# Output tiles spread between the quarter products of a two-layer encoder's feed-forward stages, and another way to the weight sums

## The chip, the core and the metric

The kernel runs on one core of a Trainium2 chip. The engines are TensorE (PE, matmuls; PEld its weight loads), VectorE (DVE), ScalarE (ACT), GpSimd (POOL) and SyncE (SP, which only issues transfers). The metric is the device time of one execution in microseconds (us); shorter is better.

## What is computed

Two layers, 512 tokens of width 1024, in fp32. Each layer is a gated feed-forward stage, a mixer of three branches, a cross-attention to 256 memory tokens, and a second feed-forward stage. Cut to the part at hand:

```python
def swiglu(h, w_in, w_out):
    a, b = jnp.split(h @ w_in, 2, axis=-1)
    return (jax.nn.silu(a) * b) @ w_out

for l in range(DEPTH):                                   # DEPTH = 2
    x = x + 0.5 * swiglu(rms_norm(x, ffn1_norm[l]), ffn1_w_in[l], ffn1_w_out[l])
    x = x + merged_branches(rms_norm(x, mix_norm[l])) @ w_mix_out[l]
    x = x + cross_attention(rms_norm(x, xattn_norm[l]), rms_norm(mem, mem_norm[l]), ...)
    x = x + 0.5 * swiglu(rms_norm(x, ffn2_norm[l]), ffn2_w_in[l], ffn2_w_out[l])
return rms_norm(x, final_norm)
```

`w_in` has 2 x 2816 columns. A *unit* is 128 columns of a with the 128 of b that belong to them, so a stage has 22 units; there are four such stages.

## The kernel before

x lies transposed in SBUF, 128 rows of the width by 512 tokens in eight tiles. Every fp32 operand of a matmul is split into a high part (a cast on ACT) and a low part (the rest, a subtraction on DVE), and `mm3` (L422) makes one product from three matmuls: high x high, high x low, low x high. For weights `Stream.split` does this, L400 on ACT and L401 on DVE, three uses ahead of TensorE (`LOOK`), into a ring of four buffers; for activations `split_to` does (L552, L553).

A stage is done in four *blocks* (`FB`): first four plain units, then three blocks of three *pairs* of units. After each block its gated products go through `w_out`: eight *output tiles*, one for each 128 rows of x, each added to x on DVE (L755). `gated` (L599) makes a plain unit's gated product: DVE L602, ACT silu L603, POOL L604, DVE L605, split.

A pair is a two-by-two block product done with seven products in place of eight; each is 4 x 2 weight tiles by 256 tokens, and so 24 matmuls. They are named after their weights: S1, A11, A12, S2, S3, A22, S4. The activations' sums are made once a stage in `combos` and `in_place` (L620, L630, splits L552 and L553). The weights' sums are made by transfers that add to what lies in SBUF, issued by POOL: S1 and S3 when the pair is loaded (L377, L378), S2 when the split of S1 has read the buffer, and S4 when that of S2 has (both L407, in the same buffer). A pair's weights come as two chunks of 1 MB. Pairs take turns between two places: the two `stage` buffers, which also hold the weights of output tiles and of all other products, and two slots of their own (`side`). `room` lets a chunk be loaded when a buffer of its place is free. The pair's results are put together by DVE additions (L663), silu (L667), a DVE product (L674) and a split.

Instructions of one engine run in the order in which a scheduler put them when the kernel was built; it starts from the order of the code and pulls work forward by its own estimates. Side tasks are advanced by `tick`, once for each gated unit, pair and output tile. Transfers of one queue (SP's, POOL's) start in order. `mem_stats` (a side task) computes the memory's norm row in the first stage's last block.

Of the kernel before, what the change touches and what calls it, by code (L numbers as in the profile page):

```python
# [14 lines left out]
P = 128  # L15
# [10 lines left out]
FB = ((4, 0), (0, 3), (0, 3), (0, 3))  # L26
# [45 lines left out]

def plan():

    out = []

    def add(key, parts, make):
        out.append((key, parts, make))

# [12 lines left out]
    def ffn(l, w_in, w_out):  # L92
        j = 0
        for b, (nc, npair) in enumerate(FB):
            j0 = j
            for _ in range(nc):
                first = l == 0 and j == 0 and w_in == "ffn1_w_in"
                add((w_in, l, j), [256, 256, 512, 1024] if first else [1024, 1024], block(w_in, l, 0, KD, (j * P, D_FF + j * P), P))
                j += 1
            for i in range(npair):  # L100
                a, g = (j * P, j * P + P), (D_FF + j * P, D_FF + j * P + P)
                side = (npair - i) % 2
                add((w_in, l, "P", j, side), [2048], blocks(w_in, l, [(0, c) for c in a] + [(4, c) for c in a]))
                add((w_in, l, "Q", j, side), [2048], blocks(w_in, l, [(4, c) for c in g] + [(0, c) for c in g]))
                j += 2
            for m in range(KD):
                add((w_out, l, b, m), [(j - j0) * P], block(w_out, l, j0, j - j0, (m * P,), P))
# [46 lines left out]
    return out  # L154


def pack(w):

    f = {n: np.asarray(a) for n, a in w.items()}
    wts = np.concatenate([np.ascontiguousarray(mk(f)).reshape(-1) for _, _, mk in plan()])  # L160
# [116 lines left out]
def emit(tc, wts, par, rows, ws_t, bd, xt, memt, const, out):  # L277
    nc = tc.nc
    pe, act, dve, pool, sp = nc.tensor, nc.scalar, nc.vector, nc.gpsimd, nc.sync
    chunks = plan()  # L280
# [37 lines left out]
    class Stream:  # L318
# [4 lines left out]

        PAIR = ("S1", "A11", "A12", "S2", "S3", "A22", "S4")

        def __init__(self):
            self.parts = []
            off = 0
            self.off = []
            for i, (key, cols, _) in enumerate(chunks):  # L330
                self.off.append(off)
                off += sum(cols) * P
                if key[2:3] == ("P",):
                    self.parts += [(i, nm, 1024) for nm in self.PAIR]
                elif key[2:3] != ("Q",):
                    c0 = 0
                    for n in cols:
                        self.parts.append((i, c0, n))
                        c0 += n
# [5 lines left out]
            self.slots = None  # L345
# [38 lines left out]
        def source(self, i, nm):  # L384

            p, q = self.loaded[i], self.loaded[i + 1]
            if nm in ("S1", "S2", "S4"):
                return self.xs[self.side(i)].f
# [1161 lines left out]
```

## Time and profile before

| | |
|---|---|
| time, median of 3 runs | 2733.13 us (2726.06 to 2738.3) |
| the profiled execution | 2724.87 us, its span 2723.0 us |
| PE busy | 2609.5 us (96%), 14790 matmuls |
| DVE busy | 1712.8 us (63%) |
| ACT busy | 1306.0 us (48%) |
| POOL busy | 398.5 us (15%) |
| granted TensorE clock, mean | 0.978 of full speed |

The span is the time from the first to the last instruction of the profiled execution. Busy shares are means over the whole span; the stages differ, and the rows below go by stages. In a timeline row the bracket gives the engine's idle time before the instruction and what ended it. PEclk is the clock that was granted to TensorE, 1.00 being the full 2.4 GHz and 0.50 the lower level.

### The profile page before, as it was taken

What the parts mean: (1) busy time and instruction counts of PE and PEld (TensorE: products, weight loads), DVE (VectorE), ACT (ScalarE), POOL (GpSimd) and SP (SyncE); (2) the same over time, 40 slices, a digit from 0 to 9 for tenths busy, and PEclk for the clock granted to TensorE, in tenths of its full rate; (3) what the DMA queues carried; (4) which work ended last, traced back from release to release, by engine and by line L of the source; (5) the groups of instructions that cost most, each with busy time, mean ns of one, the idle gap of its engine ahead of it and who ended that gap; (6) DMA issues with size and microseconds to landing.
All of it is one profiled execution on the core that took longest, in us unless ns stands there. A gap on an engine that the chain in (4) does not pass through costs nothing. (4 is left out here: it accounts for less than half of the span.)

```text
span 2723.0 us, 36733 instructions
## 1 busy us (share of the span) xinstructions
PE 2609.5 (96%) x14790; PEld 2286.3 (84%) x14790; DVE 1712.8 (63%) x2400; ACT 1306.0 (48%) x1829; POOL 398.5 (15%) x366
## 2 busy tenths in 40 slices
PE   8988999999999999899998989999999999999898
PEld 6978988878888889798888889887888888897897
DVE  7646576776656576555675556767675655765555
ACT  5333356876634444332443334579575444433334
POOL 1101134100121021011111101251000300210111
PEclk9989999999999999899999999999999999998999
DMA  5756542222233336566627666322223333376662
GB/s 187 181 153 172 150 149 85 70 78 78 89 105 124 130 106 155 154 163 172 173 74 173 176 151 156 124 86 65 90 78 95 107 125 116 101 182 160 165 150 79
DMA packets 85146, 349.11 MB, mean 128 GB/s; under 512 B 9072, under 2 KB 14832, under 8 KB 66800
## 3 DMA queue, kind: packets, MB, share of 16 engines
q1 hardware_dynamic: 63520, 269.18, 29.1%
q0 software_dynamic: 20736, 75.51, 16.0%
q8 instruction: 115, 1.88, 0.3%
q10 hardware_dynamic: 720, 2.09, 0.2%
q14 instruction: 55, 0.45, 0.1%
HBM read 344.65 MB, written 2.10 MB: 127 GB/s over the span
## 5 line engine op out<-in xcount | busy, mean ns | idle before, releaser
L423 PE MATMUL ps<-slot,whi 128*128 128x256 f32 (+1 forms) x2438 | 829.8, 341 | 80.7 <-ACT slot L552 52.3
L425 PE MATMUL ps<-slot,wlo 128*128 128x256 f32 (+1 forms) x2438 | 825.5, 339 | 6.4 <-DVE wlo L401 6.4
L424 PE MATMUL ps<-slot,whi 128*128 128x256 f32 (+1 forms) x2438 | 827.4, 339 | 1.2 <-DVE slot L553 1.2
L400 ACT CAST whi<-stage 128x1024 fp32r<-128x1024 f32 (+3 forms) x410 | 388.2, 952 | 586.6 <-PE ps L424 381.6
L423 PE MATMUL ps<-xh,whi 128*128 128x512 f32 (+1 forms) x1760 | 597.9, 340 | 5.6 <-DVE slot L1196 3.3
L401 DVE TENSOR_TENSOR wlo<-stage,whi 128x1024 fp32r<-128x1024 f32 (+3 forms) x410 | 466.2, 1139 | 215.3 <-ACT whi L400 213.4
L425 PE MATMUL ps<-xh,wlo 128*128 128x512 f32 (+1 forms) x1760 | 594.5, 338 | 1.1 <-DVE wlo L401 1.1
L424 PE MATMUL ps<-xl,whi 128*128 128x512 f32 (+1 forms) x1760 | 594.8, 338 | 0.3 <-DVE xl L487 0.3
L423 PEld LDWEIGHTS ps<-slot,whi 128*128 128x128 f32 x2438 | 474.4, 195 | 134.4 <-ACT slot L552 57.8
L425 PEld LDWEIGHTS ps<-slot,wlo 128*128 128x128 f32 x2438 | 474.0, 194 | 55.1 <-DVE wlo L401 8.8
L424 PEld LDWEIGHTS ps<-slot,whi 128*128 128x128 f32 x2438 | 474.4, 195 | 52.6 <-DVE slot L553 6.3
L400 ACT CAST whi<-slot 128x1024 fp32r<-128x1024 f32 x204 | 212.0, 1047 | 438.5 <-DMA slot<-in_wts 246.3
L401 DVE TENSOR_TENSOR wlo<-slot,whi 128x1024 fp32r<-128x1024 f32 x204 | 248.6, 1222 | 262.2 <-ACT whi L400 262.0
L423 PEld LDWEIGHTS ps<-xh,whi 128*128 128x128 f32 x1760 | 334.4, 190 | 43.5 <-DVE slot L1196 4.9
L425 PEld LDWEIGHTS ps<-xh,wlo 128*128 128x128 f32 x1760 | 334.4, 190 | 36.8 <-DVE wlo L401 1.7
L424 PEld LDWEIGHTS ps<-xl,whi 128*128 128x128 f32 x1760 | 334.5, 190 | 35.6 <-DVE xl L487 1.6
L552 ACT CAST slot<-slot 128x512 fp32r<-128x512 f32 (+2 forms) x165 | 106.2, 651 | 198.5 <-DVE slot L674 87.9
L755 DVE SCALAR_TENSOR_TENSOR x<-ps,x 128x512 f32<-128x512 f32 x129 | 87.8, 685 | 167.1 <-PE ps L425 166.9
L663 DVE TENSOR_TENSOR slot<-ps,slot 128x512 f32<-128x512 f32 x252 | 168.5, 684 | 24.1 <-PE ps L425 23.2
L407 POOL DMA_DIRECT2D slot<-in_wts x72 | 65.3, 907 | 701.0 <-DVE wlo L401 700.0
L553 DVE TENSOR_TENSOR slot<-slot,slot 128x512 fp32r<-128x512 f32 (+2 forms) x165 | 124.2, 761 | 43.2 <-ACT slot L552 42.2
L553 DVE TENSOR_TENSOR slot<-ps,slot 128x512 fp32r<-128x512 f32 (+1 forms) x144 | 92.6, 654 | 39.3 <-ACT slot L552 38.6
(208 smaller groups left out, 2639.4 us busy)
## 6 DMA issues: line engine op xcount, KB each, us to landing
stage<-in_wts SPq DMA_DIRECT2D x92, 1024.0 KB, 4.8
slot<-in_wts POOLq DMA_DIRECT2D x132, 512.0 KB, 6.2
slot<-in_wts SPq DMA_DIRECT2D x48, 1024.0 KB, 6.2
stage<-in_wts SPq DMA_DIRECT2D x77, 512.0 KB, 3.5
stage<-in_wts SPq DMA_DIRECT2D x96, 384.0 KB, 3.4
slot<-in_wts SPq DMA_DIRECT2D x36, 512.0 KB, 3.6
stage<-in_wts SPq DMA_DIRECT2D x33, 256.0 KB, 2.6
stage<-in_wts POOLq DMA_DIRECT2D x12, 512.0 KB, 8.3
```

Of the source, the lines that this page charges most:

```text
L400: mark["whi"] = act.copy(hi[:, 0:n], t).ins
L401: dve.tensor_tensor(lo[:, 0:n], t, hi[:, 0:n].bitcast(F32), op=ALU.subtract)
L407: pool.dma_start(out=t, in_=self.dram(i, int(c0 == "S2")), accum_op=ALU.add)
L423: pe.matmul(ps, lhsT=ah, rhs=bh, start=start, stop=False)
L424: pe.matmul(ps, lhsT=ah, rhs=bl, start=False, stop=False)
L425: pe.matmul(ps, lhsT=al, rhs=bh, start=False, stop=stop)
L552: act.copy(hi, src)
L553: return dve.tensor_tensor(lo, src, hi.bitcast(F32), op=ALU.subtract).ins
L663: dve.tensor_tensor(r.f, ps, other.f, op=op)
L755: dve.scalar_tensor_tensor(x[:, m, cs], ps, 0.5, x[:, m, cs], op0=ALU.mult, op1=ALU.add)
```

## The change

A stage's order is now a list, `ffn_order`: four plain units, two of their output tiles, then nine pairs in blocks of three, two, two and two. The remaining output tiles of a block stand between the products of the next block's pairs, two to a pair in the first three pairs (after S2 and A22), four to a pair after that (after A11, S2, S3 and A22). The last block's eight tiles stand alone at the end. There are five blocks of output tiles in place of four, 40 additions to x a stage in place of 32, and the same matmuls. The weights of two output tiles come in one chunk.

Pairs no longer use the stage buffers. Three slots hold six buffers of 128x1024: X0 and X1 (in turns by pair), S3, A11, A12 and A22. `fetch` fills one: S1 and S3 by a transfer from SP and one from POOL that adds, the others by one from SP. In X the sum S1 is made into S2 by a DVE addition of A11 after A11's split, and into S4 by one of A12 after S2's. Each buffer is refilled for the next pair as soon as it has been read. A pair moves 3.5 MB in place of 4.5. In-place splits start when the plain units are done, and all side work of `combos` is drained ahead of the first pair.

```diff
-FB = ((4, 0), (0, 3), (0, 3), (0, 3))
+NPLAIN = 4
+PAIR_BLOCKS = (3, 2, 2, 2)
+AHEAD = 2
+PER_PAIR = (2, 2, 2, 4, 4, 4, 4, 4, 4)
+PRODUCTS = ("S1", "A11", "A12", "S2", "S3", "A22", "S4")
+OUT_AT = {2: ("S2", "A22"), 4: ("A11", "S2", "S3", "A22")}
...
+def ffn_order():
+    o = [("unit", j) for j in range(NPLAIN)] + [("block", 0)]
+    ready = [("out", 0, m) for m in range(KD)]
+    o += [ready.pop(0) for _ in range(AHEAD)]
+    i = 0
+    for b, n in enumerate(PAIR_BLOCKS):
+        for _ in range(n):
+            for nm in PRODUCTS:
+                o.append(("product", i, nm))
+                if nm in OUT_AT[PER_PAIR[i]]:
+                    o.append(ready.pop(0))
+            i += 1
+        assert not ready
+        o.append(("block", b + 1))
+        ready = [("out", b + 1, m) for m in range(KD)]
+    return o + ready
...
         def load(self, parts=None, between=None, eng=sp):
...
-            if chunks[i][0][2:3] == ("Q",):
-                s = self.xs[self.side(i)].f
-                eng.dma_start(out=s, in_=self.dram(i, 1))
-                pool.dma_start(out=s, in_=self.dram(i, 0), accum_op=ALU.add)
-                pool.dma_start(out=t[:, 1024:2048], in_=self.dram(i - 1, 0), accum_op=ALU.add)
...
+            while self.n_load < len(chunks) and self.paired(self.n_load):
+                self.n_load += 1
+
+        def open_pairs(self):
+            self.bufs = [get(4) for _ in range(3)]
+            self.buf = dict(zip(("X0", "X1", "S3", "A11", "A12", "A22"),
+                                (r.f[:, h * 1024:h * 1024 + 1024] for r in self.bufs for h in range(2))))
...
+        def fetch(self, nm):
+            n = self.next[nm]
+            self.next[nm] += 1
+            if n == sum(PAIR_BLOCKS):
+                return
...
+            a11, a12, a22, a21 = (src[:, h * 1024:h * 1024 + 1024] for h in range(4))
+            if nm in ("S1", "S3"):
+                t = self.buf[f"X{n % 2}" if nm == "S1" else nm]
+                sp.dma_start(out=t, in_=a21)
+                pool.dma_start(out=t, in_=a22 if nm == "S1" else a11, accum_op=ALU.add)
+            else:
+                sp.dma_start(out=self.buf[nm], in_={"A11": a11, "A12": a12, "A22": a22}[nm])
 
         def split(self):
...
-            elif pair and c0 in ("S1", "S2"):
-                pool.dma_start(out=t, in_=self.dram(i, int(c0 == "S2")), accum_op=ALU.add)
...
+            elif c0 == "A11":
+                dve.tensor_tensor(x0, x0, self.buf["A11"], op=ALU.add)
+                self.fetch("A11")
+                self.fetch("S1")
+            elif c0 == "S2":
+                dve.tensor_tensor(x0, x0, self.buf["A12"], op=ALU.add)
+                self.fetch("A12")
+            elif c0 in ("S3", "A22"):
+                self.fetch(c0)
...
         def combos():
+            ws.open_pairs()
+            ws.fetch("S1")
...
+            total("S3", b12, b22, ALU.subtract)[0].free()
+            while not done:
                 yield
+            in_place("A11", 0, 0)
+            xn[0].free()
+            yield
+            in_place("A12", 1, 0)
+            total("A22", b21, c2, ALU.subtract)[0].free()
+            t2.free()
+            yield
+            in_place("S4", 1, 1)
...
+        def out_tile(b, m):
...
+                for k in range(nj):
+                    c = slice(k * P, (k + 1) * P)
+                    gh, gl, _ = gs[b][k]
+                    mm3(ps, hi[:, c], lo[:, c], gh[:, cs], gl[:, cs], k == 0, k == nj - 1)
+                dve.scalar_tensor_tensor(x[:, m, cs], ps, 0.5, x[:, m, cs], op0=ALU.mult, op1=ALU.add)
...
+        for kind, i, *rest in FFN_ORDER:
...
+            elif kind == "out":
+                out_tile(i, rest[0])
+            else:
+                if rest[0] == PRODUCTS[0]:
+                    if i == 0:
+                        drain()
+                    run = pair()
+                    next(run)
+                run.send(product(i, rest[0]))
```

VectorE's order at the end of the second stage's first block of pairs, before. L663, L674 and L553 finish the last pair, L755 adds output tiles to x, `wlo<-stage` are low parts of output weights:

```order
L663 TENSOR_TENSOR slot_9236<-ps,slot_8237 128x512
L553 TENSOR_TENSOR slot_1767<-slot_8237,slot_1767 128x2x256
L401 TENSOR_TENSOR wlo<-stage,whi 128x768
L674 TENSOR_TENSOR slot_9236<-slot_9236 128x512
L553 TENSOR_TENSOR slot_1767<-slot_9236,slot_1767 128x2x256
L755 SCALAR_TENSOR_TENSOR x<-ps,x 128x512
L401 TENSOR_TENSOR wlo<-stage,whi 128x768
L755 SCALAR_TENSOR_TENSOR x<-ps,x 128x512
L401 TENSOR_TENSOR wlo<-stage,whi 128x768
L755 SCALAR_TENSOR_TENSOR x<-ps,x 128x512
L401 TENSOR_TENSOR wlo<-stage,whi 128x768
L755 SCALAR_TENSOR_TENSOR x<-ps,x 128x512
```

The same place after, in the fourth pair (L754, L778, L603 finish a pair, L728 adds an output tile, L445 splits weights, L456 is one of the new weight sums):

```order
L754 TENSOR_TENSOR slot_8574<-ps,slot_8409 128x512
L445 TENSOR_TENSOR wlo<-slot_8269,whi 128x1024
L778 TENSOR_TENSOR slot_8409<-slot_8409,slot_8574 128x512
L728 SCALAR_TENSOR_TENSOR x<-ps,x 128x512
L445 TENSOR_TENSOR wlo<-stage,whi 128x768
L603 TENSOR_TENSOR slot_9255<-slot_8409,slot_9255 128x2x256
L754 TENSOR_TENSOR slot_8574<-ps,slot_8409 128x512
L445 TENSOR_TENSOR wlo<-slot_8042,whi 128x1024
L778 TENSOR_TENSOR slot_8574<-slot_8574 128x512
L445 TENSOR_TENSOR wlo<-slot_8268,whi 128x1024
L603 TENSOR_TENSOR slot_9255<-slot_8574,slot_9255 128x2x256
L456 TENSOR_TENSOR slot_8268<-slot_8268,slot_8042 128x1024
```

What stood behind the pair, the output tiles and their weights, now stands within the next one, and an addition of 128x1024 has come in.

TensorE's order behind the plain units of the second stage, before, with buffer numbers (`ps_8453`, `ps_8466` and `ps_8510` are the first three output tiles, `slot4_6491` holds the last two units' gated products):

```order
L425 MATMUL ps_8453<-slot4_6491,wlo_8345 128x512
L423 MATMUL ps_8466<-slot4_6491,whi_8386 128x512
L423 MATMUL ps_8453<-slot4_6491,whi_8344 128x512
L424 MATMUL ps_8466<-slot4_6491,whi_8386 128x512
L425 MATMUL ps_8466<-slot4_6491,wlo_8387 128x512
L423 MATMUL ps_8466<-slot4_6491,whi_8386 128x512
L423 MATMUL ps_8510<-slot8_1767,whi_8416 128x512
L424 MATMUL ps_8510<-slot8_1767,whi_8416 128x512
L425 MATMUL ps_8510<-slot8_1767,wlo_8417 128x512
```

After (`ps_8499` and `ps_8522` are the two output tiles ahead of the pairs, `ps_8543` is the first pair's S1, `slot2_7446` holds the last two units' gated products):

```order
L474 MATMUL ps_8522<-slot2_7446,whi_8423 128x512
L475 MATMUL ps_8522<-slot2_7446,wlo_8424 128x512
L473 MATMUL ps_8499<-slot2_7446,whi_8381 128x512
L473 MATMUL ps_8522<-slot2_7446,whi_8423 128x512
L473 MATMUL ps_8543<-slot1_3975,whi_8453 128x256
L474 MATMUL ps_8543<-slot1_3975,whi_8453 128x256
L475 MATMUL ps_8543<-slot1_3975,wlo_8454 128x256
```

Ahead of the low part of the last unit's gated product, which stands in the matmuls of L424, there stood a third output tile, and there now stands part of S1.

## Rows read from the trace of the kernel before

**Rows 1.** Feed-forward stages: length, busy PE, PEld, DVE, ACT, POOL, PEclk, DMA, GB/s.
```profile
7.24:398.63 391.39, 362.06 (x2236) 325.45 (x2237) 251.77 (x323) 163.24 (x215) 53.02 (x53) 0.95 0.61 165
986.44:1367.42 380.98, 356.96 (x2236) 323.50 (x2234) 234.25 (x279) 147.46 (x185) 52.73 (x51) 0.96 0.60 156
1367.42:1744.43 377.01, 357.03 (x2235) 324.09 (x2234) 237.91 (x302) 148.57 (x186) 49.89 (x49) 0.96 0.56 145
2332.16:2705.71 373.55, 353.89 (x2235) 321.45 (x2233) 226.74 (x269) 144.50 (x182) 48.08 (x48) 0.97 0.54 138
```

**Rows 2.** The same view: one pair, eight output tiles, and one low-clock stretch.
```profile
1053.39:1073.54 20.15, 20.15 (x169) 20.15 (x168) 11.45 (x13) 7.95 (x9) 4.31 (x5) 1.00 0.88 222
...
1711.76:1744.43 32.67, 32.67 (x146) 27.04 (x145) 28.00 (x52) 19.66 (x28) 9.18 (x7) 1.00 0.49 161
...
1339.95:1343.35 3.40, 3.40 (x10) 2.62 (x9) 2.90 (x5) 2.90 (x4) 0.66 (x1) 0.50 0.29 88
```

**Rows 3.** Waits of PE over the span: in total, times, longest.
```profile
PE ps L423 <- ACT slot L552: 52.3, 13, 7.8
PE ps L423 <- ACT whi L400: 28.6, 9, 6.3
```

**Rows 4.** Timeline of ACT and PE at one block end (start, length).
```profile
1105.95 1.04 ACT L400 CAST whi<-slot 128x1024 fp32r<-128x1024 f32 x1 [8.42 <-DMA slot<-in_wts]
...
1107.05 0.58 PE L423 MATMUL ps<-slot,whi 128*128 128x256 f32 x1 [4.55 <-ACT whi L400]
...
1127.29 0.83 ACT L400 CAST whi<-stage 128x768 fp32r<-128x768 f32 x1 [9.67 <-DMA stage<-in_wts]
...
1133.90 0.80 PE L423 MATMUL ps<-slot,whi 128*128 128x512 f32 x1 [7.30 <-ACT slot L552]
```

**Rows 5.** DMA issues of the page: KB each, median us to landing.
```profile
slot<-in_wts POOLq DMA_DIRECT2D x132, 512.0 KB, 6.2
```

**Rows 6.** Groups of instructions by line and shape: busy us, mean ns of one.
```profile
L401 DVE TENSOR_TENSOR wlo<-slot,whi 128x1024 fp32r<-128x1024 f32 x204 | 248.6, 1222 | 262.2 <-ACT whi L400 262.0
...
L663 DVE TENSOR_TENSOR slot<-ps,slot 128x512 f32<-128x512 f32 x252 | 168.5, 684 | 24.1 <-PE ps L425 23.2
...
L755 DVE SCALAR_TENSOR_TENSOR x<-ps,x 128x512 f32<-128x512 f32 x127 | 86.9, 689 | 165.7 <-PE ps L425 165.5
...
L553 DVE TENSOR_TENSOR slot<-slot,slot 128x1024 fp32r<-128x1024 f32 x20 | 26.0, 1301 | 3.3 <-ACT slot L552 3.3
```

**Rows 7.** Timeline of PE, VectorE and ACT around the first output tiles, second stage.
```profile
1030.49 0.39 PE L423 MATMUL ps<-slot,whi 128*128 128x512 f32 x1
...
1031.16 0.69 DVE L401 TENSOR_TENSOR wlo<-stage,whi 128x512 fp32r<-128x512 f32 x1 [0.46 <-ACT whi L400]
...
1033.80 0.62 ACT L552 CAST slot<-slot 128x512 fp32r<-128x512 f32 x1 [0.25 <-DVE slot L605]
...
1035.95 0.69 DVE L553 TENSOR_TENSOR slot<-slot,slot 128x512 fp32r<-128x512 f32 x1
...
1036.69 0.50 PE L424 MATMUL ps<-slot,whi 128*128 128x512 f32 x1 [0.34 <-DVE slot L553]
```

**Rows 8.** Timeline of PE and ACT at the third stage's last block.
```profile
1711.76 0.40 PE L423 MATMUL ps<-slot,whi 128*128 128x512 f32 x1
...
1715.57 0.62 ACT L552 CAST slot<-slot 128x512 fp32r<-128x512 f32 x1 [1.10 <-DVE slot L674]
```

**Rows 9.** Timeline of PE, first stage: first output tile, and the memory row.
```profile
56.00 0.39 PE L423 MATMUL ps<-slot,whi 128*128 128x512 f32 x1
...
384.06 0.48 PE L461 MATMUL ps<-slot,ones_r 128*128 128x256 f32 x1 [2.38 <-ACT slot L552]
```

**Rows 10.** Timeline of POOL and VectorE in the first stage's last block.
```profile
393.13 1.52 POOL L496 TENSOR_TENSOR nacc<-nacc,slot 128x512 f32<-128x512 f32 x1 [2.48 <-ACT slot L495]
...
393.42 1.78 DVE L487 SCALAR_TENSOR_TENSOR xl<-x,par,xh 128x512 fp32r<-128x512 f32 x1
...
396.86 0.74 DVE L487 SCALAR_TENSOR_TENSOR xl<-x,par,xh 128x512 fp32r<-128x512 f32 x1
```

More of the change, by code (lines that the diff above doesn't have):

```diff
@@ L1 @@
+from bisect import bisect_left as bisect
 import numpy as np
@@ L70, with add @@
 BRANCH_ORDER = branch_order()
+def ffn_order():
[14 more added lines that the diff above has]
+    return o + ready
+FFN_ORDER = ffn_order()
+BLOCK_AT = [0, NPLAIN]
+for _n in PAIR_BLOCKS:
+    BLOCK_AT.append(BLOCK_AT[-1] + 2 * _n)
 def plan():
-    out = []
-    def add(key, parts, make):
+    out, order = [], []
+    def add(key, parts, make, now=True):
+        i = len(out)
         out.append((key, parts, make))
+        uses = [(i, sum(parts[:k]), n) for k, n in enumerate(parts)]
+        if now:
+            order.extend(uses)
+        return i, uses
     def block(name, l, k0, nk, cols, n):
@@ L607, in gated @@
             t.free()
[L608 removed]
+            gs[-1].append((g.r[:, 0:512], g.r[:, 512:1024], g))
         xn = []
@@ new lines, in combos @@
+            xn[1].free()
+        def out_tile(b, m):
+            nj = BLOCK_AT[b + 1] - BLOCK_AT[b]
+            last = b == len(PAIR_BLOCKS)
+            hi, lo = ws.take((w_out, l, b, m // 2))
+            tail = last and m == KD - 1 and isinstance(nxt, FinalNorm)
+            for h in range(2 if tail else 1):
+                cs = slice(h * 256, h * 256 + 256) if tail else slice(0, 512)
+                ps = bank()[:, 0:cs.stop - cs.start]
+                for k in range(nj):
[3 more added lines that the diff above has]
+                dve.scalar_tensor_tensor(x[:, m, cs], ps, 0.5, x[:, m, cs], op0=ALU.mult, op1=ALU.add)
+                if tail:
+                    nxt.half(h)
+            if last and not tail:
+                nxt.tile(m)
+            if m == KD - 1:
+                for _, _, g in gs[b]:
+                    if g is not None:
+                        g.free()
+            tick(2 if last and norm is first else 1)
@@ new lines, in product, with add @@
+        def product(i, nm):
+            ps = bank()
+            hi, lo = ws.take((w_in, l, "pair", i), nm)
+            mh, ml, _ = mv[nm]
+            for e in range(2):
+                for k in range(4):
+                    c = slice(e * 512 + k * P, e * 512 + (k + 1) * P)
+                    mm3(ps[:, e * 256:(e + 1) * 256], hi[:, c], lo[:, c], mh[k], ml[k],
+                        e == 0 and k == 0, e == 1 and k == 3)
+            return ps
+        def add(ps, other, op=ALU.add):
+            r = get(1)
+            dve.tensor_tensor(r.f, ps, other.f, op=op)
+            return r
@@ L670, in pair, with silu @@
+        def silu(r):
+            mark["silu"] = act.activation(r.f, r.f, AF.Silu).ins
+            return r
+        def pair():
+            p5 = yield
+            q1 = get(1)
+            act.copy(q1.f, (yield))
+            a0 = silu(add((yield), q1))
+            u2 = add((yield), q1, ALU.subtract)
+            w = add(p5, u2, ALU.subtract)
+            q1.free()
+            p7 = yield
+            u3 = add(p7, u2)
+            b1 = add(p7, w, ALU.subtract)
+            u2.free()
             g = getr(4)
```

246 lines of the change are left out of this document (86 added, 160 removed).

## The prediction

> **What bounds the kernel now.** The first view read is that of busy times by stretch, one stretch for each of the four feed-forward stages, in the kernel's order of time [rows 1]. In all four TensorE (PE) is the busiest engine, 362.1 of 391.4 us in the first, and VectorE (DVE) comes second with 251.8. But each has two kinds of loss. PE sits idle for 29.3, 24.0, 20.0 and 19.7 us, 93.0 together, and PEclk, the granted clock, is 0.95 to 0.97, so a part of each stage runs at the lower of the clock's two levels (1.2 of 2.4 GHz).
>
> What such a stage costs without loss follows from two undisturbed stretches [rows 2]: a pair of units takes 20.15 us for 7 x 24 = 168 matmuls of 256 columns, 0.120 us each, and a block of eight output tiles 32.67 us for 144 of 512 columns, 0.227 us each. By the code a stage has 9 x 168 = 1512 of the first kind and 192 + 528 = 720 of the second (four plain units, and output tiles over 22 units in whatever blocks). That is 181.3 + 163.4 = 344.7 us. The four stages last 391.39 + 380.98 + 377.01 + 373.55 = 1522.9; without loss they would last 1378.8. So 144 us are lost, 93 to idle time, 51 to the lower clock. The last row of the group is one stretch at 0.50: 3.40 us, so 1.7 us of work lost. All that the change can win lies in these 144 us: it has the same matmuls.
>
> Then PE's waits [rows 3]: 52.3 us for ACT's split of a gated product (L552), in 13 waits, 28.6 us for ACT's split of weights (L400). One block end shows both [rows 4]. ACT idles 8.42 us for a transfer into a pair buffer (the accumulating one at L407, which can be issued only when the split of the earlier sum has read the buffer), and PE stands 4.55 us behind it. Then ACT idles 9.67 us for the block's output weights, which wait for one of the two stage buffers that the pairs use as well. The last product's additions and splits are queued behind that split on ACT and VectorE, and PE stands 7.30 us.
>
> **The change part by part.** *Weight sums.* S2 and S4 become VectorE additions in SBUF, so the 72 transfers of L407 go, and with them the first kind of stall, the 28.6 us of [rows 3] (9 waits, the longest 6.3). S1 and S3 stay transfers, but S1 has two buffers and is fetched a pair ahead, S3 is fetched when its buffer has been split, a whole pair before its use. An accumulating transfer lands 6.2 us after issue at the median [rows 5]; with the plain one ahead of it about twice that, 12.4. A pair with two output tiles takes 20.15 + 24 x 0.227 = 25.6 us, so I price these waits at nothing. If the cover went, PE would wait as in [rows 4] once a pair (second rival). SP's fetches wait for VectorE's addition or split; behind them in SP's queue stand the output weights, needed by ACT's split three uses later, some 8 us; what SP waits for stands earlier in VectorE's list than the work on those weights, so it does not stand long. POOL's queue holds in this stretch only the remaining transfers.
>
> *VectorE pays for it.* The nearest row for an addition of 128x1024 with two SBUF inputs is the split at 1.30 us [rows 6]. Per pair VectorE then does 7 splits at 1.22 (8.6), 2 additions (2.6), 7 additions from PSUM at 0.684 (4.8), 2 products and 2 splits of 128x512 like the one at 0.69 [rows 7] (2.8), and for two output tiles of four units 2 x (0.69 + 0.69) = 2.8 (such a split and the addition to x): 21.6 of PE's 25.6 us. Three splits are in hand ahead of PE, so I cost this at nothing in the steady pairs. Eight more output additions a stage (40, not 32) are 5.5 us of VectorE, inside the same cover.
>
> *Block ends.* Blocks 0 to 3 now have the next block's products between their output tiles. The last product's chain (4.43 us to its high part, [rows 8]) has the next pair's S1 and A11 before it, 2 x 2.88 us. Output weights have the stage buffers to themselves. These stalls go. What is late next:
>
> First, block 0. Before, the first tiles wait for unit 3's gated product: from the block's start at 1030.49 its high part is there at 3.93 us, its low part at 6.15 us, and PE stood 0.34 us for it [rows 7]. After, ACT splits 1024 columns of pair weights ahead of the silu in place of 512, 1.04 us in place of 0.62 [rows 4, 7], 0.42 later: 4.4 and 6.6. PE has two tiles with 9 matmuls each ahead (4.1 us), then two high products and ten of S1 (0.45 + 1.2), so it idles 0.3 + 0.5 us. Behind that VectorE has three sums and their splits, 3 x (1.22 + 1.30) = 7.6 us by the same rows, before the pair is in step: counting its list up, the low weights of S2 come some 1 us late. I take 2 us a stage; bounds 0 and 4.2 (the low part at 6.6 with one tile's 2.4 us ahead of it).
>
> Second, the last block, which has no pair behind it. There the high part came at those 4.43 us; PE now has 12 to 17 matmuls ahead of it, 2.7 to 3.9 us, in place of 24. I take 1 us a stage, bounds 0 and 1.7. Some of these eight places will also drop the clock; I take half of them, 4 x 1.7 = 7 us in all, bounds 0 and 14.
>
> Third, things that stay: the first stage's start, 48.8 us to 56.00 where 192 x 0.227 = 43.6 would do (5.2 us lost), and the memory statistics' row in its last block, 2.4 us idle [rows 9] and 1.7 for the clock. The last block shrinks from 32.7 to 21.8 us while the layer's small work after it (the recurrence's constants, the next norm) does not: I add 2 us for each first feed-forward stage, bounds 0 and 5.
>
> **The sum.** Left over: 5.2 + 4.1 + 4 x 2 + 4 x 1 + 7 + 4 = 32 us of the 144. The span falls by 112, from 2723.0 to 2611; with the 1.9 us around it (the profiled execution took 2724.9) 2613. That execution was 8.3 us below the median of the runs, so the median should be 2613 + 8 = 2621.
>
> **A rule that speaks against it.** In the first stage's last block a split on VectorE with two SBUF inputs took 1.78 us beside an addition of 1.52 us on POOL, and 0.74 us with POOL at rest [rows 10]. The Trainium skill, in "SBUF — State Buffer", section "Who interferes with whom", says that a VectorE instruction with two SBUF inputs and a GpSimd instruction that reads SBUF exclude one another; the trace agrees. In the new last block a tile lasts 12 x 0.227 = 2.72 us and holds 0.69 + 0.74 of such VectorE work and 1.52 of POOL's, 2.95 together; if they exclude one another, 32 tiles are 0.23 us late each, 7 us. If they do not, nothing is lost. This is a part of the first rival.
>
> **The rivals.** *VectorE becomes the bound.* From unit 3's end to the end of pair 2 PE has 3 x 25.6 + 5.4 = 82 us of work. VectorE has 3 x 21.6 + 7.6 + 4.5 (three operations at 0.69 of unit 3, two in-place splits at 1.22) + 2.8 = 79.7. Against it: 79.7 is still less, and on average it is at 84%. For it: its list is in order and waits for ACT and PE now and then. If it runs 5% over in each stage, 4 x 4 us, and the last block by POOL's 7, and the clock drops twice more a stage (4 x 2 x 1.7 = 14), that is 37 us more: median 2658. Chance 0.22.
>
> *The wait for transfers moves into every pair* (slower). Four buffers, S3, A11, A12 and A22, are single now, where each pair of a block had its own set before; a refill starts only after VectorE has read the buffer and then queues in SP. If one refill a pair comes late by a stall like those of [rows 4], 4.55 us and 1.7 for the clock, 36 pairs lose 225 us in place of 144: median 2733 + 81 = 2814. It decides from some 4 us a pair, that is when a refill needs over 25 us, against 12.4 in the trace, and the bytes per pair fall from 4.5 to 3.5 MB. Chance 0.03.
>
> *Only the transfer stalls go.* If the block ends merely move (the out tiles of a block stand among products which themselves wait in order), the 52.3 us of [rows 3] stay, with a drop of clock for each of 13 waits, 22 us: median 2621 + 74 - 19 (what the sum already has for such places) = 2676. Against it: the products between need nothing of the last pair. Chance 0.06.
>
> **How the numbers follow.** The forecast has 0.69. Faster by over 0.5% (14 us, about what a measurement tells from no change) holds in it and in the first and third rival: 0.97, of which I take 0.02 off for what I have not seen. The low end is the sum with the fixed 5.2 + 4.1 = 9.3 us alone: 2621 - 23 = 2598, less a little. The upper bounds of the four estimated terms (8.8 + 2.8 + 7 + 6 = 25 more) give 2646, the first rival 2658: the high end is 2662.
>
> **What would show it.** In the profile after: PE idle in each stage under 12 us, PEclk 0.98 or more, no wait of ACT for a pair transfer above 2 us; PE's waits for L552's split few, at block 0 and the last block alone; VectorE at about 84% in the first three pairs. PE waiting for VectorE's low weights all through pairs 0 to 2 would speak for the first rival, ACT waiting for transfers in each pair for the second. The forecast is wrong if the four stages together stay above 1450 us.

## The result and the profile after

The changed kernel takes 2608.6 us (median of four runs, 2607.4 to 2610.5) against 2729.6 us for the kernel before (2724.0 to 2738.3). The ratio is 0.9555, 95% interval [0.9526, 0.9583]: 121 us or 4.4% faster. The forecast was 2621 us, in a range from a little under 2598 to 2662. The profiled execution has a span of 2606.5 us.

The stretches of busy time are the rows that answer to [rows 1], one for each feed-forward stage (columns as there):

```profile
7.14:369.86 362.72, 353.56 (x2236) 320.20 (x2237) 273.41 (x340) 165.85 (x221) 35.93 (x34) 0.99 0.51 150
957.84:1305.39 347.55, 346.56 (x2235) 316.63 (x2234) 259.35 (x310) 149.65 (x191) 34.93 (x31) 1.00 0.51 141
1305.39:1654.20 348.81, 346.70 (x2236) 316.66 (x2234) 262.89 (x322) 150.44 (x192) 33.75 (x30) 1.00 0.47 131
2242.64:2589.05 346.41, 345.43 (x2235) 315.78 (x2233) 252.36 (x303) 147.51 (x190) 31.46 (x28) 1.00 0.44 122
```

PE idles 9.2, 1.0, 2.1 and 1.0 us (length less busy time), in place of 93.0 together, and PEclk, the granted clock, is 0.99 to 1.00. The four stages last 1405.5 us in place of 1522.9, 26.7 more than the 1378.8 without loss. VectorE (DVE) does 9 to 11% more in each, and it costs nothing that these rows show.

PE's waits are those of [rows 3] (in total, times, longest). L602 is the split of gated products that was L552, L444 the split of weights that was L400:

```profile
PE ps L473 <- ACT slot L602: 6.9, 6, 2.5
PE ps L511 <- ACT slot L602: 5.6, 2, 3.6
PE ps L473 <- ACT xh L536: 3.3, 2, 1.9
PE ps L473 <- DVE slot L1256: 3.3, 2, 1.6
```

The 52.3 us for the gated split are 6.9, with 0.9 more for its low part on VectorE, and no wait for the split of weights is left. The L511 waits are the memory statistics' row (3.6) and the final norm.

The page's DMA issues (KB each, median us to landing) show what went: the 72 accumulating transfers of L407 are no longer among POOL's, and the pairs' weights come in 180 plain transfers of 512 KB. The 72 that are left are the second halves of S1 and S3.

```profile
slot<-in_wts SPq DMA_DIRECT2D x180, 512.0 KB, 4.2
...
slot<-in_wts POOLq DMA_DIRECT2D x72, 512.0 KB, 6.1
```

### The profile page after: what moved, and what is told of

Same layout as the page of the kernel before. It is cut to its first block, busy times and chain, and to the rows that moved or that the text cites. A ratio compares the mean times of both kernels' runs of the same rounds, so it can differ in the third digit from the quotient of the medians.

```text
span 2606.5 us, 36643 instructions
## 1 busy us (share of the span) xinstructions
PE 2571.5 (99%) x14784; PEld 2260.2 (87%) x14784; DVE 1826.2 (70%) x2536; ACT 1321.3 (51%) x1861; POOL 337.2 (13%) x294
## 4 chain that ended last, share of the span: by engine, by line
PE 90%; ACT 5%; DVE 3%; DMA 1%; POOL 1%; issue 1%; DVEq 0%; ACTq 0%; SPq 0%; POOLq 0%
PE ps L474 29%; PE ps L473 29%; PE ps L475 29%; PE ps L1132 1%; PE ps L1120 1%; PE ps L1103 1%; ACT whi L444 1%; DVE wlo L445 1%; DVE slot L603 0%; DMA x<-in_xt 0%; DVE xl L537 0%; POOL slot L654 0%; ACT L909 0%; ACT L919 0%; PE ps L1433 0%
## 5 line engine op out<-in xcount | busy, mean ns | idle before, releaser
L473 PE MATMUL ps<-slot,whi 128*128 128x256 f32 (+1 forms) x2436 | 812.9, 335 | 6.9 <-ACT slot L602 6.9
L474 PE MATMUL ps<-slot,whi 128*128 128x256 f32 (+1 forms) x2436 | 814.3, 334 | 0.9 <-DVE slot L603 0.9
L475 PE MATMUL ps<-slot,wlo 128*128 128x256 f32 (+1 forms) x2436 | 810.9, 334 | 0.0
L444 ACT CAST whi<-stage 128x1024 fp32r<-128x1024 f32 (+3 forms) x394 | 346.4, 881 | 509.5 <-PE ps L474 412.9
L445 DVE TENSOR_TENSOR wlo<-stage,whi 128x1024 fp32r<-128x1024 f32 (+3 forms) x394 | 415.5, 1056 | 148.0 <-ACT whi L444 145.3
L473 PEld LDWEIGHTS ps<-slot,whi 128*128 128x128 f32 x2436 | 463.1, 190 | 54.0 <-ACT slot L602 10.0
L474 PEld LDWEIGHTS ps<-slot,whi 128*128 128x128 f32 x2436 | 463.7, 190 | 46.0 <-DVE slot L603 2.4
L475 PEld LDWEIGHTS ps<-slot,wlo 128*128 128x128 f32 x2436 | 463.1, 190 | 46.2
L444 ACT CAST whi<-slot 128x1024 fp32r<-128x1024 f32 x252 | 265.3, 1053 | 433.4 <-PE ps L474 318.5
L445 DVE TENSOR_TENSOR wlo<-slot,whi 128x1024 fp32r<-128x1024 f32 x252 | 307.8, 1222 | 66.0 <-ACT whi L444 66.0
L754 DVE TENSOR_TENSOR slot<-ps,slot 128x512 f32<-128x512 f32 x252 | 170.6, 689 | 140.9 <-PE ps L475 139.7
L428 POOL DMA_DIRECT2D slot<-in_wts x72 | 62.9, 874 | 1204.3 <-DMA slot<-in_wts 1053.3
L602 ACT CAST slot<-slot 128x512 fp32r<-128x512 f32 (+2 forms) x165 | 106.0, 649 | 147.3 <-POOL slot L1290 44.6
L728 DVE SCALAR_TENSOR_TENSOR x<-ps,x 128x512 f32<-128x512 f32 (+1 forms) x161 | 110.5, 686 | 88.7 <-PE ps L475 88.6
L603 DVE TENSOR_TENSOR slot<-slot,slot 128x512 fp32r<-128x512 f32 (+2 forms) x165 | 123.0, 754 | 51.7 <-ACT slot L602 51.7
L603 DVE TENSOR_TENSOR slot<-ps,slot 128x512 fp32r<-128x512 f32 (+1 forms) x144 | 92.8, 655 | 38.7 <-ACT slot L602 38.1
```

The source lines that it names most:

```text
L428: pool.dma_start(out=t, in_=a22 if nm == "S1" else a11, accum_op=ALU.add)
L444: mark["whi"] = act.copy(hi[:, 0:n], t).ins
L445: dve.tensor_tensor(lo[:, 0:n], t, hi[:, 0:n].bitcast(F32), op=ALU.subtract)
L473: pe.matmul(ps, lhsT=ah, rhs=bh, start=start, stop=False)
L474: pe.matmul(ps, lhsT=ah, rhs=bl, start=False, stop=False)
L475: pe.matmul(ps, lhsT=al, rhs=bh, start=False, stop=stop)
```

## The experiments

The change has three parts: S2 and S4 summed by VectorE, own buffers for the pairs' weights, and the spread order. What goes with the buffers was not taken apart from them: earlier fetches, output weights two tiles to a chunk, chunks loaded as far ahead as there is room, later in-place splits, side work drained ahead of the first pair. "Own buffers" stands for all of these below. They were undone one at a time and two at a time. "Grouped" is the order of before, three blocks of three pairs, each followed by its eight output tiles.

**The order alone undone** (`grouped`).

```
-PAIR_BLOCKS = (3, 2, 2, 2)
+PAIR_BLOCKS = (3, 3, 3)
...
+    for b, n in enumerate(PAIR_BLOCKS):
+        for _ in range(n):
+            o += [("product", i, nm) for nm in PRODUCTS]
+            i += 1
+        o.append(("block", b + 1))
+        o += [("out", b + 1, m) for m in range(KD)]
```

> The kernel after, with the order of before: three blocks of three pairs, each followed by its eight output tiles (the first two begun on the earlier units), block 0's eight tiles ahead of the first pair. Buffers and weight sums stay those of after. Theory A (own buffers for the pair weights are what ends the block-end waits, since the last product's additions and splits no longer queue behind a split that waits for output weights): the waits for the gated product's split stay away from the ends of blocks 1 and 2, about 2610 to 2630 us, ratio 0.955 to 0.963. Theory B (spreading the tiles is what ends them): 52 us of such waits and 22 us of lower clock come back, about 2676 us, ratio 0.98.

2598.3 us (2598.0 to 2601.0), ratio 0.9522 [0.9508, 0.9537]. Theory B falls: without the spread no block end came back, and the kernel is faster than theory A had it. It is 10 us faster than the changed one. The two were timed apart and the intervals of their ratios overlap a little; kernels of either order that were timed side by side follow below. PE's waits in this trace:

```profile
PE ps L506 <- ACT slot L597: 4.3, 2, 2.9
...
PE ps L468 <- ACT slot L597: 1.3, 4, 0.7
```

L597 is the gated split: 1.3 us where before had 52.3 in the same order of products and tiles.

**The VectorE sums alone undone** (`transfer_sums`).

```
+            elif c0 == "S1":
+                pool.dma_start(out=x0, in_=self.quarter(i, 0), accum_op=ALU.add)
...
-                dve.tensor_tensor(x0, x0, self.buf["A12"], op=ALU.add)
+                pool.dma_start(out=x0, in_=self.quarter(i, 1), accum_op=ALU.add)
```

> The kernel after, with S2 and S4 made by accumulating transfers again, issued when S1 and S2 have been split (72 transfers of 512 KB back, 72 additions of VectorE gone). Order and buffers stay those of after. If the transfers are hidden behind the four splits between (some 11 us for 6.2 us of transfer), the time stays: 2600 to 2615 us, ratio 0.953 to 0.958, and VectorE is 10 points less busy in the first three pairs. If these transfers were a cause of their own, ACT waits for them as before: 28.6 us of PE's waits and half as much for the clock, about 2650 us, ratio 0.971.

2660.1 us, ratio 0.9741 [0.9726, 0.9756]: the transfers are not hidden, and cost a little more than the second case had. The timeline of VectorE, POOL, ACT and PE shows one such place in the second stage (start, length, engine and line, in brackets the idle time before and what ended it):

```profile
1067.88 1.22 DVE L449 TENSOR_TENSOR wlo<-slot,whi 128x1024 fp32r<-128x1024 f32 x1
...
1074.16 0.86 POOL L428 DMA_DIRECT2D slot<-in_wts  x1 [8.64 <-DMA slot<-in_wts]
1074.76 1.15 POOL L456 DMA_DIRECT2D slot<-in_wts  x1
...
1085.83 1.04 ACT L448 CAST whi<-slot 128x1024 fp32r<-128x1024 f32 x1 [12.67 <-DMA slot<-in_wts]
...
1086.93 0.58 PE L479 MATMUL ps<-slot,whi 128*128 128x256 f32 x1 [3.16 <-ACT whi L448]
```

The first row is the low split of S1, done at 1069.1. From then on the sum for S2 (L456) could have been issued. It was issued at 1074.76, because POOL's queue stood 8.64 us at an accumulating fetch (L428) that waits for its plain half. Two accumulating transfers then ran at once. ACT could go on only at 1085.83, 16.7 us after the split, and PE stood 3.16 us behind it.

**Order and sums undone, own buffers kept** (`grouped_transfer_sums`: both edits).

> Both undone at once: the order of before and S2 and S4 by accumulating transfers; only the own buffers for pair weights and the earlier fetches stay of the change. Theory A (own buffers are enough): 2610 to 2640 us, ratio 0.956 to 0.967. Theory B (the spread order removes the block ends, the VectorE sums the transfers' waits): near before, 2690 to 2730 us, ratio 0.985 to 1.0.

2763.4 us, ratio 1.0129 [1.0107, 1.0151]: slower than before, outside both cases. PE's waits:

```profile
PE ps L474 <- ACT whi L443: 85.3, 20, 7.6
PE ps L476 <- DVE wlo L444: 11.2, 21, 0.8
PE ps L474 <- ACT slot L603: 7.0, 9, 2.4
```

They are waits for the split of pair weights, in the middle of blocks, and only 7.0 us are for gated products. The row of events of `transfer_sums` stands here too (POOL):

```profile
1081.11 0.87 POOL L423 DMA_DIRECT2D slot<-in_wts  x1 [6.69 <-DMA slot<-in_wts]
1081.71 1.15 POOL L451 DMA_DIRECT2D slot<-in_wts  x1
```

The split of S1 was done at 1077.6. The transfer for S2 (L451) was issued 4.2 us later, behind a fetch (L423) that had waited for its plain half.

**The VectorE sums alone done** (`before_vector_sums`, on the kernel before).

```
             elif pair and c0 in ("S1", "S2"):
-                pool.dma_start(out=t, in_=self.dram(i, int(c0 == "S2")), accum_op=ALU.add)
+                h = int(c0 == "S2")
+                dve.tensor_tensor(t, t, self.loaded[i][:, h * 1024:(h + 1) * 1024], op=ALU.add)
```

> The kernel before with one edit: S2 and S4 are made by a VectorE addition of A11 and A12, where before accumulating transfers made them. Order and shared buffers of before stay. With it the runs so far form a square: shared or own buffers, transfers or VectorE. If the accumulating transfers behind the splits of S1 and S2 were the whole cause: 2600 to 2620 us, as the grouped order with own buffers (2598), ratio 0.953 to 0.96. If own buffers are needed as well (pairs and output weights still share the stage buffers, ACT waits 124 us for them in before): 2640 to 2690 us, ratio 0.967 to 0.985.

2628.9 us, ratio 0.9654 [0.9627, 0.968], between the two cases. Two lines bring 99 of the change's 119 to 121 us. PE's and ACT's waits, two views:

```profile
PE ps L424 <- ACT slot L553: 18.5, 10, 3.0
```

```profile
ACT whi L400 <- DMA stage<-in_wts: 70.1, 28, 5.1
```

ACT's waits for transfers in the kernel before were these:

```profile
ACT whi L400 <- DMA slot<-in_wts: 246.3, 52, 10.1
ACT whi L400 <- DMA stage<-in_wts: 124.1, 34, 9.7
```

The 246.3 us for pair buffers are gone. The waits for the stage buffers fell too, though the buffers are shared as before. What is left of the block ends is of this kind (ACT and PE, second stage):

```profile
1094.89 0.83 ACT L400 CAST whi<-stage 128x768 fp32r<-128x768 f32 x1 [4.64 <-DMA stage<-in_wts]
...
1098.03 0.50 PE L424 MATMUL ps<-slot,whi 128*128 128x512 f32 x1 [2.70 <-ACT slot L553]
```

It is the second stall of [rows 4] (9.67 and 7.30 us there): the output weights wait for a stage buffer, and PE for the gated split behind them. With own buffers, and what goes with them, it is gone: in `grouped` PE's waits for the gated split are 1.3 us. Together (ratio to before):

| | S2, S4 by transfers | by VectorE |
|---|---|---|
| shared buffers, grouped | 2729 us, 1 (before) | 2628.9, 0.9654 |
| own buffers, grouped | 2763.4, 1.0129 | 2598.3, 0.9522 |
| own buffers, spread | 2660.1, 0.9741 | 2608.6, 0.9555 (after) |

The spread order is worth 103 us where the transfers remain. There PE's waits for the split of weights fall from 85.3 to 12.5 us, while those for gated products rise from 7.0 to 20.2. That the output tiles between a pair's products give the transfers more time fits this, but no run shows it by itself. With VectorE's sums the spread order brings nothing.

**The transfers' wait made on purpose** (`single_x`).

```
-                self.fetch("A11")
-                self.fetch("S1")
+                self.fetch("A11")
...
+            elif c0 == "S4":
+                self.fetch("S1")
```

> The kernel after with one buffer for the sums S1, S2 and S4 in place of two: the next pair's S1 is fetched only when S4 has been split. This makes the wait of the prediction's second rival on purpose: plain and accumulating transfer, some 12 us, against about 8 us of PE's work between the split of S4 and the use of S1. If the price stands as that rival had it, 4 to 5 us and 1.7 us for the clock in each of 36 pairs: 2780 to 2850 us, ratio 1.02 to 1.045. If it is hidden: 2605 to 2620 us, ratio 0.955 to 0.96.

2807.9 us, ratio 1.0291 [1.0274, 1.0309], as the first case had it. It is 199 us over the changed kernel, 5.5 in each of 36 pairs.

```profile
PE ps L474 <- ACT whi L444: 119.9, 39, 9.3
```

**VectorE made dearer** (`vector_plus`; `vector_plus_half` has it for the second sum alone).

```
                 dve.tensor_tensor(x0, x0, self.buf["A11"], op=ALU.add)
+                dve.tensor_tensor(x0, x0, self.buf["A11"], op=ALU.subtract)
+                dve.tensor_tensor(x0, x0, self.buf["A11"], op=ALU.add)
```

> The kernel after with VectorE's weight sums made dearer: each is followed by a subtraction and an addition of the same quarter (2 x 1.22 us more per sum, 4.9 us per pair), the values stay. From the first pair to the end of the third VectorE is busy 72 of 83 us in the second stage of after; 14.7 us more make 86.7. If only the excess over PE's time counts: 3.7 us a stage, 15 in all, 2610 to 2635 us, ratio 0.956 to 0.965. If VectorE's own waits in its ordered list can't be used up, all of it shows: 4 x 14.7 = 59 us, about 2668 us, ratio 0.977. If it has room to spare: 2605 to 2612 us.

> Half the dose: only the second sum of a pair is followed by a subtraction and an addition (2.4 us more per pair). VectorE then has 72 + 7.3 = 79.3 of 83 us in the first three pairs. If only the excess over PE's time counts: no change, 2605 to 2615 us, ratio 0.955 to 0.958. If all of it shows: 4 x 7.3 = 29 us, about 2638 us, ratio 0.966.

2615.0 us, ratio 0.9582 [0.9564, 0.96], and 2610.6 us, ratio 0.9562 [0.9541, 0.9582]: most of the added work is hidden. Both times lie in the ranges of the case in which only the excess over PE's time counts. First the three pairs of the second stage in the changed kernel:

```profile
1011.50:1037.00 25.50, 25.50 (x193) 24.51 (x192) 25.50 (x30) 13.65 (x17) 1.76 (x2) 1.00 0.52 144
1037.00:1063.00 26.00, 26.00 (x197) 25.02 (x196) 20.93 (x26) 11.20 (x14) 1.73 (x2) 1.00 0.74 189
1063.00:1089.00 26.00, 26.00 (x197) 25.02 (x196) 20.06 (x25) 11.19 (x15) 1.73 (x2) 1.00 0.65 176
```

then with the full dose:

```profile
1018.00:1044.00 26.00, 25.39 (x191) 24.18 (x190) 26.00 (x30) 11.83 (x14) 0.88 (x1) 1.00 0.42 122
1044.00:1070.00 26.00, 26.00 (x198) 25.02 (x197) 26.00 (x32) 11.07 (x14) 2.61 (x3) 1.00 0.68 178
1070.00:1096.00 26.00, 26.00 (x198) 25.02 (x197) 25.05 (x31) 12.12 (x16) 1.73 (x2) 1.00 0.70 186
```

VectorE is busy for all of the first pair in the changed kernel, and has room in the two after it (80 and 77%). With the dose it is full for two pairs and 96% busy in the third, and PE loses 0.61 us. So the 59 us that VectorE's list gained in the first three pairs of the four stages (4 x 14.7) moved the time by 6. Of these, 3.9 lie ahead of the pairs: at the first stage's block 0 PE waits 6.48 us for the gated split, where it waited 2.54 in the changed kernel. Two of the added operations (L453, L454) stand in VectorE's list between the steps of the last unit (VectorE and PE, full dose):

```profile
61.86 1.22 DVE L453 TENSOR_TENSOR slot<-slot,slot 128x1024 f32<-128x1024 f32 x1
...
63.60 1.22 DVE L454 TENSOR_TENSOR slot<-slot,slot 128x1024 f32<-128x1024 f32 x1
...
68.33 1.22 PE L477 MATMUL ps<-slot,whi 128*128 128x512 f32 x2 [6.48 <-ACT slot L606]
```

In the steady pairs VectorE sets no end, at block 0 it does.

**Where the spread order loses.** Five kernels looked for the 10 us between the two orders. `spread_from_block1` writes block 0's tiles ahead of the first pair (`OUT_AT` has an empty entry for 0 besides):

```
-AHEAD = 2
-PER_PAIR = (2, 2, 2, 4, 4, 4, 4, 4, 4)
+AHEAD = KD
+PER_PAIR = (0, 0, 0, 4, 4, 4, 4, 4, 4)
```

> The kernel after with all eight output tiles of block 0 ahead of the first pair; later blocks stay spread. Theory C (the 10 us that the spread order costs against the grouped one lie in the two places where it leaves PE too little work: the first tiles of block 0 and the last block): half of it goes, mostly the first stage's 2.54 us gap and 1.7 us of clock and 0.5 to 1 us in each other stage, 2601 to 2605 us, ratio 0.953 to 0.9545. Rival (the spread costs everywhere, by VectorE or transfers beside the tiles): 2606 to 2610 us.

2605.2 us, ratio 0.956 [0.9539, 0.9582]: the two cases meet there, so it decides nothing. Block 0's waits in stages two to four fell from 0.98 to 0.53 us, in the first stage the wait grew to 3.24.

`spread_mended` has two edits more:

```
-OUT_AT = {... 4: ("A11", "S2", "S3", "A22")}
+OUT_AT = {... 4: ("A11", "S2", "A22", "S4")}
...
         split_to(o.r[:, 0:MEM], o.r[:, MEM:2 * MEM], a)
+        yield
+        yield
         row_scale(mem_row, [o.r[:, 0:MEM], o.r[:, MEM:2 * MEM]])
```

> The same, and the last of four tiles of a block behind product S4 rather than A22, so that the last block's first tile has a tile of the block before between it and the last product's additions, and two more steps of the output tiles between the split of the memory statistics and PE's matmul on it (3.55 us of PE's wait in after). Theory C: the waits at the last blocks (1.22 and 1.14 us) and the 3.55 us with 1.7 us of clock go as well, 2593 to 2599 us, ratio 0.950 to 0.9525. Rival (they move to the next place in order): 2600 to 2606 us.

2604.6 us (2602.6 to 2605.6), ratio 0.9554 [0.9533, 0.9576]. The last blocks' waits are gone from the trace, but the memory row kept 3.06 and 1.05 us, and theory C's time was not reached. The same two steps on the grouped order (`grouped_late_row`):

> The kernel with the grouped order, own buffers and VectorE sums (2598.3 us), and the same two steps between the split of the memory statistics and the matmul on it, 2.87 and 0.95 us of PE's waits there. If these waits and the lower clock behind them cost what they show: 2592 to 2595 us, ratio 0.949 to 0.951. If the wait moves on to the row's next use: 2597 to 2599 us.

2597.2 us (2593.9 to 2600.5), ratio 0.953 [0.951, 0.955]: not to be told from `grouped`. The row's waits fell from 2.87 and 0.94 to 1.41 and 1.14 us. It ran beside `spread_mended`, and no run of the one reaches the other: the grouped order is the faster by about 7 us.

Last, the begun tiles. In before the first two output tiles of a block start on its earlier units, and `grouped` had kept that. `grouped_whole_tiles` takes it away:

```
-            if m == 0:
-                for e in range(2):
-                    begun[e] = (bank(), ws.take((w_out, l, b, 0)))
-                    partial(*begun[e], b, whole, range(nj - 2))
...
+            w = ws.take((w_out, l, b, m // 2))
```

> The grouped kernel (2598 us) without the one thing that it shares with before beyond its order: the first two output tiles of a block are no longer begun on the block's earlier units ahead of the last product's results; every tile is written whole. Theory D (a begun tile and a spread tile are two covers for the same 4.4 us between the last product and the high part of its gated units, so that spreading had nothing left to cover): waits at all twelve block ends, some 1 to 1.7 us each and part of them with a drop of clock, 2612 to 2630 us, ratio 0.957 to 0.9635. Rival (the order between matmuls of ready tiles takes care of it anyway): 2597 to 2603 us, ratio 0.951 to 0.954.

2598.6 us (2594.2 to 2599.1), ratio 0.9529 [0.9514, 0.9543]. Theory D falls for the twelve blocks of pairs: no wait of 0.4 us or more stands at their ends. At the first stage's block 0 it holds: `grouped` has 0.73 us there, and without the begun tiles it is this, with a lower clock behind:

```profile
62.21 0.80 PE L468 MATMUL ps<-slot,whi 128*128 128x512 f32 x1 [3.29 <-ACT slot L597]
```

```profile
62.20:65.60 3.40, 3.39 (x8) 2.71 (x9) 3.37 (x4) 0.00 (x0) 0.00 (x0) 0.50 0.03 11
```

The time doesn't show it, and the trace says why: the memory row's waits of 2.87 and 0.94 us are missing in it, so that one loss is made up by another gain. `spread_begun` gives begun tiles to block 0 of the mended spread kernel:

> The mended spread kernel (2604.6 us), with the two begun tiles of before at block 0 alone. If the first stage's block 0 (3.33 us of wait, 1.7 us of clock) is what still parts it from the grouped order: 2596 to 2600 us, ratio 0.950 to 0.9525. If the begun tiles change nothing there: 2603 to 2606 us.

2604.0 us (2599.8 to 2606.7), ratio 0.9547 [0.9531, 0.9563]: they change nothing, and block 0's wait in the first stage stays at 3.35 us. The profiles of these two differ by 9.2 us at the same point behind the first stage (PE's wait for L1258, or L1272, the same instruction), and by under 2 after it. The stretch from 340 to 370 us, which holds the first stage's last block, has most of it; first `grouped_whole_tiles`, then `spread_begun`:

```profile
340.00:370.00 30.00, 30.00 (x135) 24.86 (x134) 27.13 (x45) 17.93 (x28) 13.72 (x12) 1.00 0.35 120
```

```profile
340.00:370.00 30.00, 25.36 (x100) 20.06 (x100) 27.68 (x48) 20.70 (x36) 15.15 (x15) 0.89 0.47 163
```

```profile
362.95 0.58 PE L511 MATMUL ps<-slot,ones_r 128*128 128x256 f32 x1 [3.76 <-ACT slot L602]
364.41 0.58 PE L511 MATMUL ps<-slot,ones_r 128*128 128x256 f32 x1 [0.88 <-DVE slot L603]
```

The memory statistics' matmul has 4.6 us of waits here and a lower clock behind them (a clock of 0.89 over 30 us is 3.3 us of work), 8 us together; in the other it waits for nothing. This is no mark of the order: in `grouped` the same row has 2.87 and 0.94 us with a clock of 0.50 behind, more than the 3.55 us and one drop of the changed kernel.

What parts the changed kernel from `grouped` lies in every stage. From its first output tile to its last, each stage is longer by 4.2, 1.2, 2.4 and 1.3 us (first stage, `grouped`, then the changed kernel):

```profile
56.40:365.90 309.50, 304.61 (x2042) 282.09 (x2041) 237.85 (x291) 137.54 (x175) 29.02 (x29) 0.99 0.52 142
```

```profile
55.93:369.63 313.70, 306.31 (x2042) 282.69 (x2041) 234.92 (x290) 137.84 (x181) 28.03 (x28) 0.99 0.49 137
```

The places where PE idles more are block 0 (2.54 us and a drop of the clock in the first stage, against 0.73) and the last blocks (1.22 and 1.14 us, against less than 0.4). In `spread_mended` the last blocks' waits are gone. Its span is still 7.4 us longer than that of `grouped`, and 5.0 of these have gathered by PE's first wait behind the first stage (for L1256 at 525.13 us, and for the same instruction at 520.17). Block 0's wait of 3.33 us, against 0.73, lies ahead of that point. Why the begun tiles cover block 0 in the grouped order and not in the spread one was not found.

## Why the prediction was right, and where its reason was not

**The lossless time and the leftover.** 32 us were forecast to stay of 144, 26.7 did:

| term | forecast | measured in the trace after |
|---|---|---|
| start of the first stage | 5.2 | 5.2 |
| memory row, with its clock | 4.1 | 3.55 + 1.7 |
| block 0, four stages | 8 | 2.54 + 0.99 + 0.97 + 0.98 = 5.5 |
| last block, four stages | 4 | 1.22 + 1.14 = 2.4 (none in stages two and four) |
| other drops of the clock | 7 | 1.7 (one, behind block 0 of the first stage) |
| small work of the layer | 4 | 6.7, all that remains, not located |

Each term but one lies within its bounds; the memory row, which had none, is 1.2 over. The last row is only what is left: 2.1, 1.9, 2.0 and 0.7 us in the four stages, so it isn't the layer's small work alone, which was priced for two of them (4 us, bounds 0 and 10). That the sum comes out is in part luck, since drops of the clock forecast at 7 were 1.7. Behind the stage's start there are two low-clock stretches; the first is at the lower level, as in [rows 2]:

```profile
64.00:67.40 3.40, 3.40 (x13) 2.88 (x12) 3.31 (x5) 1.59 (x2) 0.00 (x0) 0.50 0.00 0
```

**From span to median.** The span came 4.5 us below the 2611 forecast. The other 8 us of the 12 between forecast and result are the step from the profiled execution to the median: the prediction carried over the 8.3 us by which the execution of before lay under its median. After, the profiled execution took 2608.4 and the median is 2608.6, so this step was wrong.

**Weight sums: the mis-sized term.** The prediction gave the sums the 28.6 us of [rows 3] that PE waits for the split of weights. Alone, with order and buffers of before, they bring 99 us. They take away those waits, and 33.8 of the 52.3 us for gated splits as well, with the clock behind both. The prediction had put those 52.3 us down to the block ends.

**Block ends: the step that failed.** "Blocks 0 to 3 now have the next block's products between their output tiles ... These stalls go." They go, but not by that. The grouped order with own buffers and VectorE sums has 1.3 us of them in place of 52.3, and is 7 to 10 us faster than the spread one; the spread order with the transfers still has 20.2. Of the 52.3 us the VectorE sums alone take 33.8, with the stage buffers shared as before. The other 18.5 go with the own buffers, as the sentence right behind the one quoted says: "Output weights have the stage buffers to themselves." [Rows 4] held this too: PE's 7.30 us follow ACT's 9.67 us for a stage buffer. Where ACT's split isn't late, the last product's additions run in time in either order. The third rival ("only the transfer stalls go", 2676) rests on the same mistake: it kept the 52.3 us if the order did not act.

**VectorE.** 84% was forecast for the first three pairs, 85.8% was measured in the second stage (66.49 of 77.5 us), though not evenly: the first pair has no room at all. The first rival was further off than its chance of 0.22 said, since 59 us more on VectorE in those pairs cost 6. Its part on POOL shows in the trace. In the first stage's last block the same VectorE split took 1.76 us beside an addition on POOL and 0.74 us with POOL idle (POOL idled 4.11 us up to 352.05):

```profile
350.41 0.74 DVE L537 SCALAR_TENSOR_TENSOR xl<-x,par,xh 128x512 fp32r<-128x512 f32 x1
...
363.00 1.76 DVE L537 SCALAR_TENSOR_TENSOR xl<-x,par,xh 128x512 fp32r<-128x512 f32 x1
```

```profile
352.05 1.52 POOL L546 TENSOR_TENSOR nacc<-nacc,slot 128x512 f32<-128x512 f32 x1 [4.11 <-ACT slot L545]
...
355.25 0.74 POOL L1346 TENSOR_TENSOR slot<-slot 128x256 f32<-128x256 f32 x1 [0.53 <-ACT slot L1345]
...
357.66 1.24 POOL L1346 TENSOR_TENSOR slot<-slot 128x256 f32<-128x256 f32 x1
...
362.77 1.44 POOL L546 TENSOR_TENSOR nacc<-nacc,slot 128x512 f32<-128x512 f32 x1 [0.85 <-ACT slot L545]
```

At 357.66 it is POOL that is stretched, beside VectorE's split of weights, which started at 357.64. So either of the two may be held up, as [rows 10] showed for one of them. The Trainium skill, "SBUF — State Buffer", section "Who interferes with whom", which has two-input VectorE instructions and GpSimd reads of SBUF exclude one another, agrees with these rows. (In [rows 10] POOL was not at rest through all of the 0.74 us: its next addition began at 397.22, after VectorE.) PE has no wait for VectorE in that block, so the 7 us of the first rival were not spent in the way it had them. But the addition at 357.66, 0.5 us longer than the one at 355.25, stands in the chain to the memory row: ACT's split of it waited for POOL, and PE's 3.55 us end behind that split:

```profile
358.93 0.41 ACT L602 CAST slot<-slot 128x256 fp32r<-128x256 f32 x1 [1.81 <-POOL slot L1346]
```

**Transfers in every pair.** The second rival's price was about right: 4.55 + 1.7 = 6.3 us a pair was written, 5.5 was measured where such a wait was made, on the X buffer, which the rival had not named. It did not come up in the changed kernel: no wait of PE for the weights' split is in its trace, and none of ACT for a pair buffer. So the four single buffers are refilled in time, and X is because it has two. The 12.4 us "in the trace" for a refill were an estimate; in the changed kernel a plain and an accumulating transfer land 4.2 and 6.1 us after issue, 10.3 together.

**The signs.** PE idles under 12 us in each stage, PEclk is over 0.98, ACT waits for no pair transfer, the gated split is waited for at block 0 and the last block alone, all as written.

**Which version is fastest.** Own buffers and VectorE sums in the grouped order: 2598.3 us, 0.9522 [0.9508, 0.9537], and 2597.2 with the late row.

## What to carry to other kernels

A wait is named after the instruction that PE stands at, but its cause lies at the first idle time upstream: the 52.3 us that looked like the ends of blocks began with ACT waiting for transfers and buffers. When a change has several parts, undo each and do each alone: here two lines held four fifths of the gain, and the new order of the tiles cost some 7 to 10 us. An equal time doesn't say that nothing changed: in `grouped_whole_tiles` a new wait of 3.29 us and two that were missing cancelled, and only the trace told. A transfer that can only be issued after a split has read its target must be priced with the queue that issues it, not with its landing time alone.

## What the runs showed that was not expected

- An accumulating transfer of 512 KB lands 6.1 us after issue at the median of the changed kernel; the three issued from 1070 to 1090 us in `transfer_sums`, two of them 0.6 us apart with plain ones beside them, had a median of 9.1. The queue ahead of one cost another 5.7.
- Own buffers with the old sums were slower than shared ones (1.0129): more buffers were no help where the transfer that makes the next sum stood in POOL's queue.
- A gap of PE of 2.54 us was followed by 3.4 us at a clock of 0.50. One of 1.63 us, at the same instruction of two kernels, was followed by a stretch at 1.00 in the changed kernel and by one at 0.51 in `grouped_whole_tiles`. So the price of a gap could not be read from its length alone:

```profile
524.20:527.60 3.40, 3.40 (x15) 2.83 (x16) 3.40 (x7) 3.37 (x5) 0.00 (x0) 1.00 0.08 13
```

```profile
518.50:521.90 3.40, 3.40 (x10) 2.62 (x9) 3.40 (x7) 3.37 (x5) 0.00 (x0) 0.51 0.27 55
```
